# 24 of a decoder layer's 32 gate tiles made in pairs by seven block products, in a stage of their own ahead of the heads

## The chip, the cores and the metric

The kernel runs on one core of a Trainium2 chip. The metric is the device time of one execution in microseconds (us), the median over several runs. The time before is 1961.22 us, the median of 3 runs from 1959.63 to 1961.33. A core has five engines that run side by side, each through its own queue in order: PE (matrix products, with its weight loads as PEld), DVE (VectorE), ACT (ScalarE), POOL (GpSimd) and SP, which here issues most DMAs. Products land in PSUM (8 banks); everything else lives in SBUF, and what does not fit there goes through DRAM.

## The reference

One layer of a decoder: 16 meta tokens and 1024 tokens of width 1024, a token-mixing block of two branches (gated linear attention and mLSTM), merged by two sigmoid gates, then a gated FFN with a short causal convolution. Cut to what matters here:

```python
proj = rms_norm(h) @ w_in + b_in            # 1040 x 1024 by 1024 x 8216
(g_q, g_k, g_v, g_r, g_lr, m_q, m_k, m_v, m_o, m_i, m_f, gate_a, gate_b) = split(proj)
log_a = log_sigmoid(g_lr @ gla_w_gate + gla_b_gate) / 16
o_gla = head_rms(gla_chunked(g_q * s, g_k, g_v, log_a)) * silu(g_r)
o_ml  = head_rms(mlstm_chunked(conv(m_q), conv(m_k), m_v, m_i, log_sigmoid(m_f))) * sigmoid(m_o)
y = sigmoid(gate_a) * (o_gla @ w_branch_gla) + sigmoid(gate_b) * (o_ml @ w_branch_ml)
h = h + y @ w_out
h = h + (silu(gate) * up) @ w_down          # gate, up = conv(rms_norm(h) @ w_up)
```

The gate tiles of the title are the columns of `g_r`, `m_o`, `gate_a` and `gate_b`: 4 x 1024 columns, 32 tiles of 128.

## The kernel before

**Numbers.** Each float32 operand is split into a high part (H) and a low part (L) that PE takes at full rate; a product is three matmuls, H·H, H·L and L·H. The splits cost an ACT copy (H) and a subtraction (L, DVE or POOL).

**Stages.** (1) x is loaded, normalised and transposed into `xH`, `xL` (`norm_x`), while the first projections start. (2) Eight heads, 0 to 3 GLA and 4 to 7 mLSTM. (3) The merge products (`prod3`, L951): `bg` with the GLA outputs `og`, then `bm`. (4) The output projection (`out_product`, L1235). (5) The FFN up-projection (`piece`, `product`, L1149), its convolution and gating (`gate_pair`). (6) The down-projection (`down`, L1365). Stage 5 already makes its tiles in pairs by seven block products: x in 2 x 2 blocks (4 of the 8 k blocks by half of the tokens), the two weight tiles in 2 x 2 blocks, sums of blocks prepared ahead (`combos`, `prep_pair`), then products V, X, Y, Z of 12 matmuls on 258 or 256 columns, some of them added up in one PSUM bank: V, X | Y, Z | X again | Y, Z again, the last two behind the next piece's first four. A pair is two pieces of seven products.

**Main work and side work of a head.** The main work is PE's projections: k and q in three segments each (24 matmuls on about 342 columns, `proj_cm`, L155), v in nine chunks (`proj_v`, L198 and L185, DVE adds the bias), then the gate tiles: two of r (`gate_proj`, L444) and one of gate_a (`merge_gate`, L454), three segments each. ACT evicts k, q and gates from PSUM and adds the bias; r stays in SBUF, gate_a goes to DRAM (`gsc`). After the heads the eight gate_b tiles follow, also to DRAM. The side work is a generator for each head, `gla(s)` or `mlstm(s)`, which works on the k, q and v of the head before: in GLA the decay (`pre`, three products, abs, exp, log and a scan `bc`), seven levels of scores (`level`: DVE differences, ACT exp, POOL products L663, DVE product L664; then the PE product `sc`, L600, and a masked copy by DVE or ACT copies), the chain of states over 8 chunks, and `post` (norm: a power on POOL, L93; scaling, L538; transposes `ot`, L548; the gate r applied, L550; the split of the result and its store to `osc`). `advance()` takes one step of the oldest side generator after each main segment. `small_rows` works out the mLSTM's rows for all heads, once, as a side generator behind GLA head 3.

**Order.** The framework plans the order of each engine's instructions when the kernel is built: by priority, which is the order of the code except where `hp(n)` moves a block ahead by n, and taking what is ready by its own estimate of times. On the chip the order is then fixed, and an engine waits at an instruction whose inputs or buffer are not there.

**Buffers that matter.** Weights: raw tiles in `wr` (2), splits in `wH`, `wL` (3 each). Staging `gst` (1). PSUM in the heads: `pj` 3, `s` 3, `ot` 2 banks. In the heads' pool: `k`, `q`, `v`, `r` 2 each, `w` 5, `of` and `oH` 1 each. When the heads' pool closes, its place is taken by the merge stage's `Y` and `O` tiles (`yg`, `og`).

Of the kernel before, what the change touches and what calls it, by code (L numbers as in the profile page):

```python
# [17 lines left out]
P = 128  # L18
# [27 lines left out]
def hybrid_kernel(ctx, tc, x, meta, norm_mix, w_in, b_in, gla_w_gate, gla_b_gate, gla_norm,  # L46
# [24 lines left out]
    hd = heads_ctx.enter_context(tc.tile_pool(name="hd", bufs=1, side="right"))  # L71
    ps_ctx = heads_ctx.enter_context(ExitStack())
    ps = ps_ctx.enter_context(tc.tile_pool(name="ps", bufs=1, space=PSUM))
# [33 lines left out]
    lrHL = [wp.tile([P, NK, P], F32R, name=f"w{p}_lr", tag="w" + p) for p in "HL"]  # L107
    for t in lrHL:
        nc.vector.memset(t.bitcast(F32), 0.0)
    SMALL = ((0, O_LR, 16), (32, O_MI, 4), (64, O_MF, 4))  # L110

    def prep_small():

        raw = wp.tile([P, T], F32, name="wr_lr", tag="gst", bufs=1)[:, :NK * 24].rearrange("p (k n) -> p k n", k=NK)
        wH, wL = lrHL
# [12 lines left out]
    class Units:  # L128
        def __init__(self):
            self.specs, self.got, self.done = [], {}, 0  # L130
# [5 lines left out]
        def get(self, u, ahead=2):  # L136
            while self.done <= min(u + ahead, len(self.specs) - 1):
# [7 lines left out]
    U = Units()  # L145

# [68 lines left out]
    GATE_LATER = [s < 5 for s in range(8)]  # L215

    def kq_units(s):
        if s in uk:
            return
# [6 lines left out]
    def head_units(s):  # L226
        h = s % 4
        kq_units(s)
        if s == 0:
            uk["lr"] = U.add()  # L230
        uv[s] = u_v((O_GV if s < 4 else O_MV) + DV * h, f"{'gm'[s // 4]}v{h}_")

    def gate_units(s):
        h = s % 4
        o = (O_GR if s < 4 else O_MO) + DV * h
        ur[s] = [u_cm(w_in, o + P * j, f"r{s}_{j}") for j in range(2)]

    head_units(0)
    for s in range(8):
        if GATE_LATER[s]:  # L240
            kq_units(s + 1)
        gate_units(s)
        if s < 7:
            head_units(s + 1)
        uga[s] = u_cm(w_in, O_GA + P * s, f"ga{s}")
    for j in range(NK):
# [5 lines left out]
    xM = hd.tile([P, NK * 48 + 80], F32R, name="xM")  # L252
    nc.gpsimd.memset(xM.bitcast(F32), 0.0)
    gmix = hd.tile([P, D], F32, name="gmix", tag="bc")

    rmask = hd.tile([P, T], F32, name="rmask")
    nc.vector.memset(rmask, 1.0)
    nc.vector.memset(rmask[:, 0:1], 0.0)
    nc.vector.memset(rmask[:, NM:].rearrange("p (n w) -> p n w", w=P)[:, :, 0:1], 0.0)
    A = hd.tile([P, NC, P], F32, name="A", tag="A", bufs=1)  # L260
    nc.vector.memset(A, 0.0)

# [5 lines left out]
    va = hd.tile([P, T], F32, name="va", tag="oH", bufs=1)[:, :P]  # L268
# [15 lines left out]
    wg = hd.tile([NM + 1, 512], F32, name="wg")  # L284
    small.append((wg[0:16, :], gla_w_gate[0]))
    small.append((wg[16:17, :], gla_b_gate))
    vf = hd.tile([P, T], F32, name="vf", tag="r", bufs=2)[:88, :2 * P].rearrange("p (a b) -> p a b", b=P)
    rows(vf[:, 0, :], ffn_conv_w, 0, 88)
    rows(vf[0:44, 1, :], ffn_conv_w, 88 * P, 44)
    rows(vf[44:88, 1, :], ffn_conv_b, 0, 44)  # L290

# [10 lines left out]
    def load_x(*tiles):  # L302
        for i in tiles:
            n = NM if i == 0 else P
            tag, bufs = [("w", 5), ("q", 2), ("k", 2)][(i >= 5) + (i >= 7)]
            xt = hd.tile([P, T], F32, name=f"xt{i}", tag=tag, bufs=bufs)
# [3 lines left out]
    def norm_x(i):  # L310
# [3 lines left out]
        ss = hd.tile([P, 1], F32, name=f"xss{i}", tag="ss1", bufs=3)  # L314
        junk = hd.tile([P, T], F32, name=f"xj{i}", tag="of", bufs=1)
        nc.scalar.activation(junk[:n, :D], xt[:n, :D], AF.Square, accum_out=ss[:n])
        with hp(40):
            v = hd.tile([P, 1], F32, name=f"xv{i}", tag="xv", bufs=3)
            nc.vector.tensor_scalar(v[:n], ss[:n], 1.0 / D, EPS, OP.mult, OP.add)
            rs = hd.tile([P, 1], F32, name=f"xr{i}", tag="xr", bufs=3)  # L320
# [28 lines left out]
    for i in range(4, NC + 1):  # L349
        if i == NC:  # L350
            columns()
        last = norm_x(i)
# [5 lines left out]
    fc = const.tile([P, 4, 44], F32, name="fc")  # L358

    def conv_columns():  # L360
        for i in range(2):
# [1116 lines left out]
```

## Time and profile before

| what | value |
|---|---|
| median of 3 runs | 1961.22 us (1959.63 to 1961.33) |
| the profiled execution's span | 1960.6 us |
| mean granted PE clock | 0.997 of full |
| start of the heads' main work without x tiles to wait for | about 36 us |
| first merge product | 963.65 us |
| HBM read, written | 166.07 MB, 56.71 MB |

How to read the rows that follow. In a row of stretches: from and to (us), length, then busy time and number of instructions of PE, PEld, DVE, ACT and POOL, the granted PE clock, the DMA engines' share and GB/s; with a line or tile chosen, only the engines that ran it. In a group of instructions: line, engine, operation, output<-inputs, shapes, count | busy us, mean ns | idle time before them, and what ended it. In the view of one line: count, ns min/median/max, first and last start. In a timeline: start, length, engine, line, what; in brackets the idle time before it and its releaser. In the waits: who waited for whom, us in all, times, longest. Matmuls overlap in the records (a matmul of 342 columns shows some 320 ns but the next starts 157 ns later), so stretches are used for PE.

### The profile page before, as it was taken

The numbers are of one execution on the slowest core, as the hardware profiler recorded it, in microseconds if no ns is written. First come the engines' busy times: TensorE is split into PE (matmuls) and PEld (weight loads), VectorE is DVE, ScalarE is ACT, GpSimd is POOL, SyncE is SP. The second block draws the span as 40 slices with busy tenths as digits, with TensorE's granted clock in tenths as the row PEclk, the third lists the DMA queues.
The fourth block names the chain that finished last, engine by engine and source line by source line (L and its number), as shares of the span: only waits on it lengthen the run. The fifth ranks groups of instructions, "written<-read, shape, count | busy, mean of one in ns | idle before, by whom it ended". The sixth has DMA issues, their size and how long they took to land. (4 is left out here: it accounts for less than half of the span.)

```text
span 1960.6 us, 31110 instructions
## 1 busy us (share of the span) xinstructions
PE 1925.3 (98%) x13181; PEld 1840.3 (94%) x13181; DVE 965.9 (49%) x1444; ACT 753.4 (38%) x1183; POOL 308.1 (16%) x229
## 2 busy tenths in 40 slices
PE   7999999999999999999999999999999999999998
PEld 6999999999999999999999998999999999978886
DVE  6263636264644434332112447688888888710202
ACT  5243535344634424233311235544445454431211
POOL 3030202020000000000000002012222222364220
PEclk9999999999999999999999999999999999999999
DMA  4211202131323231319952433333333333587721
GB/s 152 57 35 56 76 24 91 29 100 33 104 72 87 67 97 44 98 43 179 327 215 65 136 112 109 119 108 120 113 130 113 122 121 119 172 301 258 244 94 43
DMA packets 191270, 224.79 MB, mean 115 GB/s; under 512 B 11102, under 2 KB 150640, under 8 KB 191131
## 3 DMA queue, kind: packets, MB, share of 16 engines
q1 hardware_dynamic: 190843, 221.76, 36.1%
q8 instruction: 103, 1.69, 0.4%
q10 hardware_dynamic: 288, 1.05, 0.1%
q14 instruction: 36, 0.29, 0.0%
HBM read 166.07 MB, written 56.71 MB: 114 GB/s over the span
## 5 line engine op out<-in xcount | busy, mean ns | idle before, releaser
L1365 PE MATMUL pd<-ringH,a 128*128 128x512 f32 x416 | 131.6, 393 | 2.0 <-DMA a<-adrL 2.0
L155 PE MATMUL pj<-xH,wH_r 128*128 128x342 f32 x384 | 126.1, 328 | 0.0
L155 PE MATMUL pj<-xH,wL_r 128*128 128x342 f32 x384 | 122.9, 320 | 0.0
L155 PE MATMUL pj<-xL,wH_r 128*128 128x342 f32 x384 | 122.6, 319 | 0.0
L1399 DVE TENSOR_TENSOR acc<-pd,acc 128x512 f32<-128x512 f32 x16 | 11.1, 691 | 196.9 <-PE pd L1365 196.9
L1365 PEld LDWEIGHTS pd<-ringH,a 128*128 128x128 f32 x416 | 78.0, 188 | 20.1 <-DMA a<-adrL 2.4
L663 POOL TENSOR_TENSOR pk<-pk,kT 128x256 f32<-128x256 f32 (+1 forms) x40 | 58.8, 1501 | 163.0 <-ACT pk L661 90.5
L1365 PE MATMUL pd<-ringL,a 128*128 128x512 f32 x208 | 82.5, 397 | 1.5 <-POOL ringL L1344 1.5
L198 PE MATMUL pv<-wH_gv,xH 128*128 128x256 f32 x256 | 74.8, 292 | 0.0
L198 PE MATMUL pv<-wH_mv,xH 128*128 128x256 f32 x256 | 74.6, 291 | 0.0
L1235 PE MATMUL po<-wL_wo,yH 128*128 128x256 f32 x256 | 72.0, 282 | 2.0 <-DVE wL_wo L104 2.0
L1235 PE MATMUL po<-wH_wo,yH 128*128 128x256 f32 x256 | 72.8, 284 | 0.9 <-DVE h L1242 0.9
L155 PEld LDWEIGHTS pj<-xH,wH_r 128*128 128x128 f32 x384 | 72.3, 188 | 1.0 <-issue 1.0
L155 PEld LDWEIGHTS pj<-xL,wH_r 128*128 128x128 f32 x384 | 72.3, 188 | 1.0 <-issue 1.0
L155 PEld LDWEIGHTS pj<-xH,wL_r 128*128 128x128 f32 x384 | 72.2, 188 | 0.0
L198 PE MATMUL pv<-wL_gv,xH 128*128 128x256 f32 x256 | 72.0, 281 | 0.0
L198 PE MATMUL pv<-wL_mv,xH 128*128 128x256 f32 x256 | 71.9, 281 | 0.0
L198 PE MATMUL pv<-wH_gv,xL 128*128 128x256 f32 x256 | 71.9, 281 | 0.0
L198 PE MATMUL pv<-wH_mv,xL 128*128 128x256 f32 x256 | 71.9, 281 | 0.0
L1235 PE MATMUL po<-wH_wo,yL 128*128 128x256 f32 x256 | 71.8, 281 | 0.0
L202 DVE TENSOR_TENSOR v<-pv,bB 128x256 f32<-128x256 f32 x64 | 26.8, 420 | 87.3 <-PE pv L198 87.3
L1196 DVE SCALAR_TENSOR_TENSOR cv<-u,fc,cv 128x1024 f32<-128x1024 f32 x44 | 69.4, 1578 | 0.4
(625 smaller groups left out, 6704.3 us busy)
## 6 DMA issues: line engine op xcount, KB each, us to landing
rd<-in_ffn_w_down_dram SPq DMA_DIRECT2D x36, 512.0 KB
rg<-in_ffn_w_up_dram SPq DMA_DIRECT2D x22, 512.0 KB
ru<-in_ffn_w_up_dram SPq DMA_DIRECT2D x22, 512.0 KB
a<-adrH SPq DMA_DIRECT2D x44, 256.0 KB
a<-adrL SPq DMA_DIRECT2D x44, 256.0 KB
adrH<-aH SPq DMA_DIRECT2D x21, 512.0 KB
adrL<-aL SPq DMA_DIRECT2D x21, 512.0 KB
wr_r<-in_w_in_dram SPq DMA_DIRECT2D x16, 512.0 KB
```

The source lines that it names most:

```text
L155: nc.tensor.matmul(pt[:, :n], a[:, k, :], b[:, k, base + t0:base + t0 + n], start=(i == 0), stop=(i == 3 * NK - 1))
L198: nc.tensor.matmul(pt[:, :DV], a[:, k, t0:t0 + P], b[:, k % 4, :], start=(i == 0), stop=(i == 3 * NK - 1))
L202: nc.vector.tensor_tensor(vt[:n, c, :DV], pt[:n, :DV], bB[:n, :], OP.add)
L663: nc.gpsimd.tensor_tensor(e, e, k, OP.mult)
L1196: nc.vector.scalar_tensor_tensor(y, u[:, j:SEQ + j], fc[:, j, jj:jj + 1], y, OP.mult, OP.add)
L1235: nc.tensor.matmul(pt[:, :DV], a, b[:, k % 4, :], start=(k == 0 and i == 0), stop=(k == NK - 1 and i == len(terms) - 1))
L1365: nc.tensor.matmul(pts[t][n], a[:, c], b[:, 512 * n:512 * n + 512], start=start and i == 0, stop=stop and i == 2)
L1399: nc.vector.tensor_tensor(acc[:, h], pts[t][n], acc[:, h], OP.add)
```

## The change

The order of the kernel becomes: x; k and q of head 0; two gate_b tiles (`EARLY`); a gate stage of 12 pairs; the small projection (`lr`, for the decays and the mLSTM's gates) and v of head 0; the heads; six gate_b tiles (`LATE`) as the main work of the last head.

- **The gate stage** makes r of all eight heads (16 tiles) and gate_a (8 tiles) in 12 pairs by seven products, as the FFN does. The sums of blocks of x (`TB`) are made once ahead of it; for the rest it reads `xH`, `xL` in place. Weights are split with the three slots of `wH`, `wL` alone. The results, without bias, are stored to DRAM: r to `rdr`, gate_a to `gsc`.
- **Heads**: main work is k and q and v alone. `load_r(s)` fetches r from DRAM within the side work, and the bias is added in the sigmoid or silu (in the merge stage too). `main(gen, rate)` takes `rate` side steps a segment.
- The decay of a GLA head becomes a function of its own, `decay(s)`, called before `post` of the head before it (for head 0 ahead of its v). Scores of small levels come two levels behind their products instead of one. `post` has one more empty step, `small_rows` two more; `small_rows` runs ahead of GLA head 0.
- **Pools**: tiles that hold x live in a pool `xs` that closes after k and q of head 0; the gate stage's pool `gp` and PSUM pool `psG` follow in its place, then the heads' pool `hd`. k and q of even heads and the masks stay in `keep`. The masks are built in the gate stage, wholly on POOL.

```diff
-    GATE_LATER = [s < 5 for s in range(8)]
+    EARLY, LATE = (0, 1), (2, 3, 4, 5, 6, 7)
...
     def merge_gate(which, j):
-        u = (uga if which == "a" else ugb)[j]
-        c = (C_GA if which == "a" else C_GB) + j
-        if which == "b" and j in (1, 3):
-            st = hd.tile([P, T + 3], F32, name=f"g{which}{j}", tag="k", bufs=2)
+        if j in (3, 5):
+            st = kq_tile(8, "k")
...
-        yield from proj_cm(u, TH_POST, T0, lambda p, t0, n: nc.scalar.activation(
-            st[:, t0:t0 + n], p, AF.Identity, bias=cc(c)))
+        yield from proj_cm(ugb[j], TH_POST, T0, lambda p, t0, n: nc.scalar.activation(st[:, t0:t0 + n], p, AF.Copy))
...
+    def load_r(s):
+        heads[s]["r"] = []
+        for j in range(2):
+            r = hd.tile([P, NP], F32, name=f"r{s}_{j}", tag="r", bufs=2)
+            nc.sync.dma_start(r, rdr[2 * s + j])
+            heads[s]["r"].append(r)
...
-        pk = level(1)
-        yield
-        yield
-        for b in (2, 4, 8, 16, 32, 64):
-            nk = level(b)
...
+        pks = []
+        for b in (1, 2, 4, 8, 16, 32, 64):
+            pks.append(level(b))
+            if b > 2:
+                scores_small(pks.pop(0), b // 4)
             yield
...
+        if s < 3:
+            decay(s + 1)
+            yield
         sc = rstd_of(ss, DV, NC + 1, hd, f"rs{s}")
...
+    for _ in kq_proj(0):
+        pass
+    xs_ctx.close()
...
+    for p in range(2):
+        n = (W0, W1)[p]
+        for kk in range(2):
...
+            for dst, c0, eng in ((ra, T0 + W0 * p, nc.gpsimd), (rc, T0 + 512 + W0 * p, nc.vector)):
+                h, l = (rows(t)[:, :, :, c0:c0 + n].bitcast(F32) for t in (xH, xL))
+                eng.tensor_tensor(dst, h, l, OP.add)
+            nc.vector.tensor_tensor(t12[:, 0], rc[:, 0], ra[:, 0], OP.subtract)
+            nc.vector.tensor_tensor(t34[:, 0], rc[:, 1], rc[:, 0], OP.subtract)
+            nc.vector.tensor_tensor(t12[:, 1], rc[:, 1], t12[:, 0], OP.subtract)
+            nc.vector.tensor_tensor(t34[:, 1], ra[:, 1], t12[:, 1], OP.subtract)
+            for r0, t, eng in ((0, t12, nc.vector), (8, t34, nc.gpsimd)):
+                h, l = (rows(TB[x, p][:, r0:r0 + 8, :]) for x in "HL")
+                nc.scalar.activation(h, t, AF.Copy)
+                last = eng.tensor_tensor(l, t, h.bitcast(F32), OP.subtract)
+
+    for j in EARLY:
+        for _ in merge_gate("b", j):
+            pass
...
+    def block_weights(q):
...
+        a["A11"], a["A12"] = two(rg, "A1")
+        yield
...
+        a["S1"], a["S3"] = two(sa, "SA")
+        yield
...
+        a["S2"], a["S4"] = two(sb, "SB")
+        yield
...
+        nc.sync.dma_start(g_raw, wsrc(w_in, 4, 4, off + P, P))
+        nc.scalar.activation(t[:, 0:4], g_raw, AF.Copy)
+        nc.gpsimd.tensor_tensor(t[:, 4:8], g_raw, t[:, 0:4].bitcast(F32), OP.subtract)
+        yield
...
+    def gate_piece(q, p):
...
+            gout[q] = (gp.tile([P, 2, NA], F32, name=f"goA{q}", tag="oA", bufs=2),
+                       gp.tile([P, 2, 512], F32, name=f"goB{q}", tag="oB"))
...
+        gate_product(V, q, p, "A12", "B21", True, True)
+        gate_product(X, q, p, "A11", "B11", True, True)
+        with hp(PRI_E):
+            nc.scalar.activation(g1, V[:, :n], AF.Copy)
+            nc.vector.tensor_tensor(g1, X[:, :n], g1, OP.add)
+        yield
+        gate_product(Y, q, p, "S1", "T1", True, True)
+        gate_product(Z, q, p, "S3", "T3", True, True)
+        yield
+        gate_product(X, q, p, "S2", "T2", False, True)
+        with hp(PRI_E):
+            nc.scalar.activation(u2, X[:, :n], AF.Copy)
+            nc.vector.tensor_tensor(e2, Y[:, h2], u2[:, h2], OP.add)
+            nc.vector.tensor_tensor(e2, Z[:, h2], e2, OP.add)
+        yield
+        gate_product(Y, q, p, "S4", "B22", False, True)
+        gate_product(Z, q, p, "A22", "T4", False, True)
+        with hp(PRI_E):
+            nc.vector.tensor_tensor(e1, Y[:, h2], u2[:, h2], OP.add)
+            nc.vector.tensor_tensor(g2, Z[:, :n], u2, OP.add)
+        yield
+
+    def gate_store(q):
+        _, dst, i = GP[q]
+        oA, oB = gout.pop(q)
+        nc.sync.dma_start(dst[i:i + 2, :, 0:NA].rearrange("j p t -> p j t"), oA)
+        nc.sync.dma_start(dst[i:i + 2, :, NA:NP].rearrange("j p t -> p j t"), oB)
...
+    for q in range(len(GP)):
+        for p in range(2):
+            g = gate_piece(q, p)
+            next(g)
+            if p == 1:
+                weights_step(q + 1)
+            next(g)
+            if p == 1:
+                weights_step(q + 1)
+            if behind:
+                next(behind)
+            if p == 0 and q:
+                gate_store(q - 1)
+                weights_step(q)
+                weights_step(q)
...
+            next(g)
+            behind = g
...
-    main(head_proj(0))
-    conv_columns()
+    main(lr_proj(), 0)
     for s in range(8):
+        if s == 0:
+            decay(0)
+            side.append(small_rows())
         side.append((gla if s < 4 else mlstm)(s))
-        if s == 3:
-            side.append(small_rows())
-        nxt = head_proj(s + 1) if s < 7 else iter(())
-        if GATE_LATER[s]:
-            main(islice(nxt, 6))
-        main(gate_proj(s))
-        main(nxt)
-        main(merge_gate("a", s))
-    for j in range(NK):
-        main(merge_gate("b", j))
+        rate = (1.45, 1.7, 1.7, 1.7, 1.2, 1.2, 1.2, 1.8)[s]
+        if s == 0:
+            main(v_proj(0), rate)
+        if s < 7:
+            main(kq_proj(s + 1), rate)
+            main(v_proj(s + 1), rate)
+        else:
+            for j in LATE:
+                main(merge_gate("b", j), rate)
     while side:
         advance()
...
-        nc.scalar.activation(y, y, AF.Sigmoid)
+        nc.scalar.activation(y, y, AF.Sigmoid, bias=cc(C_GA + j))
```

More of the change, by code (lines that the diff above doesn't have):

```diff
@@ L420, in head_proj @@
             if s == 0:
[L421 to L422 removed]
+                yield from together(pk, pq)
             else:
@@ L697, in gla @@
         scores_large(pk, 64)
+        load_r(s)
         yield
@@ L830, in mlstm @@
         qh = WB
+        load_r(s)
         yield
```

312 lines of the change are left out of this document (201 added, 111 removed).

## The prediction

> **What bounds the kernel now.** I read the page's busy shares first, then the slices, then stretches of single stages.
>
> ```profile
> span 1960.6 us, 31110 instructions
> PE 1925.3 (98%) x13181; PEld 1840.3 (94%) x13181; DVE 965.9 (49%) x1444; ACT 753.4 (38%) x1183; POOL 308.1 (16%) x229
> ...
> PE   7999999999999999999999999999999999999998
> ...
> DVE  6263636264644434332112447688888888710202
> ...
> PEclk9999999999999999999999999999999999999999
> ```
>
> PE is busy in every slice at full clock, so time goes only where PE work goes, provided that no other engine takes over. A share of 98% could hide idle time inside pipelined matmuls, so I price matmuls by stretches. The first row below holds the L155 matmuls (plain projections) of the stretch that has nothing but plain gate tiles; the second, from the FFN, holds two pairs made of seven block products (2 x 168 matmuls; 338 start in it).
>
> ```profile
> 899.50:963.65 64.15, 64.15 (x408) 64.03 (x408) 1.00 1.02 261
> ...
> 1401.33:1441.41 40.08, 40.08 (x338) 40.08 (x337) 34.39 (x43) 18.97 (x25) 10.22 (x6) 1.00 0.36 119
> ```
>
> Plain: 64.15 us / 408 = 157.2 ns for 342 columns; two tiles are 144 of them, 22.64 us. By seven products, two tiles take 40.08 / 2 = 20.04 us, and the FFN keeps that pace with DVE busy 34.39 of 40.08 us.
>
> One place does lose time, at the end of head 3:
>
> ```profile
> 504.82 3.79 POOL L93 TENSOR_TENSOR rs3r<-rs3v,mhalf 128x9 f32<-128x9 f32 x1 [7.21 <-DVE rs3v L91]
> ...
> L93 POOL TENSOR_TENSOR rs2r<-rs2v,mhalf x1: 1797/1797/1797, 390.8 to 390.8; 128x9 f32<-128x9 f32 x1
> ...
> 509.05 1.59 PE L548 MATMUL ot<-ident,or 128*128 128x128 f32 x4 [3.15 <-DVE or L538]
> ...
> 505.00:510.00 5.00, 1.85 (x11) 1.23 (x9) 3.38 (x6) 4.95 (x5) 3.60 (x1) 0.82 0.00 0
> 510.00:515.00 5.00, 4.88 (x19) 4.84 (x18) 4.94 (x11) 1.10 (x2) 0.00 (x0) 0.50 0.01 4
> 515.00:520.00 5.00, 5.00 (x33) 4.80 (x33) 4.92 (x7) 1.61 (x2) 0.00 (x0) 1.00 0.75 196
> ```
>
> POOL's power for the head's norm takes 3.79 us there and 1.80 in another head; PE sits idle 3.15 us, and then the granted clock is 0.82 and 0.50 for two windows of 5 us. Lost: 3.15 + 5 x 0.18 + 5 x 0.50 = 6.6 us at most; I take 6, as some of the window at 0.82 is the idle time itself. This is also the price of a stall: beyond some 3 us it costs twice itself. The Trainium skill states the same under TensorE: Matmul & The Clock Gate, section "Part 1: The HAM clock gate": an idle window of about 3.4 us drops the array to half clock until a busy window has passed. By that rule the loss is 3.15 + 1.7 = 4.9 us, and the trace, with its longer low window, says somewhat more.
>
> **The change, part by part.**
>
> *Products.* 24 tiles at 22.64 us a pair become 12 pairs at 20.04: 12 x 2.60 = **31.2 us less** on PE. The eight remaining tiles stay plain.
>
> *Stage set-up.* The combinations of x (TB) are built in four quarters, each on 2 x 2 x 257 columns. POOL adds 1028 elements and subtracts 2056; DVE adds 1028, combines 4 x 514 and subtracts 2056; ACT copies 2 x 2056.
>
> ```profile
> L1344 POOL TENSOR_TENSOR ringL<-rd,ringH 128x1024 fp32r<-128x1024 f32 x21 | 51.4, 2460 | 37.9 <-ACT ringH L1343 37.9
> ...
> L104 DVE TENSOR_TENSOR wL_r<-wr_r,wH_r 128x1024 fp32r<-128x1024 f32 x16 | 19.5, 1218 | 5.9 <-ACT wH_r L103 5.9
> L103 ACT ACTIVATE wH_r<-wr_r 128x1024 fp32r<-128x1024 f32 x16 | 16.9, 1056 | 31.8 <-PE pv L198 18.1 <-PE pj L155 13.6
> ...
> 36.59 0.69 DVE L331 TENSOR_TENSOR xL<-xtp,xH 128x512 fp32r<-128x512 f32 x1
> ...
> 36.00:62.00 26.00, 25.88 (x218) 25.88 (x219) 4.11 (x7) 6.97 (x14) 4.37 (x8) 1.00 0.08 22
> ```
>
> At 2.46, 1.22 and 1.06 us per 1024 a quarter costs POOL 7.4, DVE 6.1 and ACT 4.2 us; all four 29.6, 24.5 and 17. What hides them: the last x tile is done at about 37, and from 36 on PE still has two thirds of the 218 matmuls above (q and k; the small projection leaves), 17 us, then two early gate tiles, 22.6, then V and X of the first piece, 2.9: 42 us until the first T block is needed, against 15 us of POOL for the first half. The second half has 10 us more. Cost 0; without the cover it would be the 30 us of POOL.
>
> *Inside the stage.* DVE has less here than in the FFN (no convolution, no gating), and that stage runs at 20.04. Two waits are new. First, three weight slots hold three splits a pair, so SB of pair q takes the slot that the product Y(S4) of pair q-1 has just left, and only Z(A22), 20.04 / 14 = 1.43 us, lies between it and X(S2), which needs the split:
>
> ```profile
> L1109 DVE TENSOR_TENSOR LSB<-SB,HSB 128x1024 fp32r<-128x1024 f32 x17 | 20.5, 1207 | 0.0
> ...
> L1108 ACT ACTIVATE HSB<-SB 128x1024 fp32r<-128x1024 f32 x17 | 18.0, 1060 | 6.5 <-PE Z L1149 6.5
> ```
>
> 1.06 + 1.21 - 1.43 = 0.84 us late, 11 times, 9 us if PE waits in place; 0 if V and X of the next piece, which are ready, are queued first. Second, oB has one buffer, so the e2 sums of pair q wait until pair q-1 is stored:
>
> ```profile
> 868.05 0.34 SPq L456 DMA_DIRECT2D gsca<-ga  x1
> ...
> 873.28 0.55 ACT L454 ACTIVATE gb<-pj,col 128x342 f32<-128x342 f32 x1 [3.06 <-DMA gsca<-ga]
> ...
> DVE of L550 <- DMA oscmL<-of: 21.8, 4, 8.2
> ```
>
> A store of 513 KB is 5.2 us from issue to release. Counted from the end of Y(S4) of q-1: e1 and g2 done at about 2.1, oA issued 2.2, oB 2.5, released 7.7, e2's first sum done 8.2; Y(S4) of q needs that bank after Z, X, V, X, Y, Z, 6 x 1.43 = 8.6. It just fits; a store as late as the 8.2 us in the last row makes it 2.6 us late. Queued behind e2 on DVE are the splits of the next weights, with 5 products of slack. I take 3 us for both waits together (0 to 10).
>
> *Into the heads.* PSUM and SBUF change hands, and the small projection runs before any decay can. Its 72 matmuls (11.4 us) hide the hand-over; the decay of head 0 (next rows: first product 90.4, scan from 98.0, 2.3 long: 10 us) hides under head 0's v, 24 us. I take 2 us (0 to 6).
>
> ```profile
> L623 PE MATMUL pre<-raw_s,wg x24: 447/450/555, 90.4 to 416.3; 17*128 17x346 f32 x16, 17*128 17x348 f32 x8
> ...
> L632 DVE TENSOR_TENSOR_SCAN bc<-rmask,la x4: 2324/2324/2325, 98.0 to 423.6; 128x1040 f32<-128x1040 f32 x4
> ```
>
> *Heads.* They keep all side work and lose nine of their 24 main segments. Both halves of GLA head 1, all engines and then L155 alone, and an mLSTM head:
>
> ```profile
> 198.90:252.00 53.10, 53.07 (x347) 51.38 (x347) 34.08 (x44) 27.66 (x39) 14.50 (x10) 1.00 0.22 60
> 252.00:306.90 54.90, 54.90 (x385) 51.76 (x383) 19.97 (x42) 20.48 (x43) 2.63 (x3) 1.00 0.20 61
> ...
> 198.90:252.00 53.10, 44.02 (x265) 41.61 (x264) 1.00 0.22 60
> 252.00:306.90 54.90, 16.11 (x96) 15.10 (x96) 1.00 0.20 61
> ...
> 525.50:623.00 97.50, 97.50 (x661) 94.39 (x661) 44.81 (x99) 41.98 (x69) 2.21 (x5) 1.00 0.34 94
> ...
> L1123 DVE TENSOR_TENSOR SA<-ru x22: 669/674/692, 1247.8 to 1664.2; 128x512 f32<-128x512 f32 x22
> ...
> L1124 DVE TENSOR_TENSOR SA<-rg,ru x22: 683/1710/1720, 1248.4 to 1665.1; 128x512 f32<-128x512 f32 x22
> ...
> PEld sc L600: 1.6, 4
> ```
>
> A GLA head keeps 108.0 - 3 x 11.32 = 74 us of PE against DVE 54.05 - 3 x 1.22 = 50.4; an mLSTM head 97.5 - 34 = 63.5 against 41. Averages still favour PE. The first half does not: its levels now lie under six segments of k and q, 6 x 44.02 / 11 = 24.0, plus 53.07 - 44.02 = 9 of side matmuls: 33 us, and DVE needs 34.08 less two gate splits, 31.6. That is 96%. The new order (scores two levels behind instead of one) gives it slack, and the second half has 39 us of PE for 19 of DVE to catch up in. I take 5 us over all heads (0 to 8 stalls like the one above, less its clock share: 0 to 25). The stall at 505 itself should go: the small rows, whose scans ran beside that power, move to head 0: **6 us less**. r comes by DMA instead of from PSUM: two loads of 513 KB, asked for steps ahead of `post`, at 60 GB/s of traffic in the rows above: 0.
>
> *End of the heads.*
>
> ```profile
> L456 SPq DMA_DIRECT2D gscb<-gb x8: 319/320/339, 883.7 to 965.2; - x8
> ...
> L935 SPq DMA_DIRECT2D ogL<-oscgL x8: 320/446/713, 924.9 to 956.4; - x8
> ...
> 963.65 0.32 PE L951 MATMUL bg<-ogH,wH_bg 128*128 128x342 f32 x1
> ```
>
> The loads of o took 32 us and were issued 39 us before the first merge product. Now the last head has 6 x 11.32 = 68 us of gates plus 14 of side matmuls, and 17 side steps at 1.8 a segment end about half-way: some 39 us remain, and the first products take k blocks as they land. 0 (0 to 12).
>
> **Sum** against the profiled span: 1960.6 - 31.2 - 6 + 3 + 2 + 5 = 1933.4; the median of the runs stands 0.6 above that span: **1934 us**.
>
> **Rivals.**
>
> *The stage's waits are real* (the oB store or the SB slot). For: one buffer, and the 8.2 us store. Against: PE's queue can take other products first, as FFN pieces already interleave. SB's 9 us and a store half as late as that row, 11 x 1.3 = 14, are 23 in place of 3: 1954 (1945 to 1957). Chance 0.18. With the store 2.6 us late each time and no SB wait, 11 x 2.6 = 29 in place of 3, it is 1960, no change (within 0.2%, 3.9 us, which is what this kernel's runs can tell): 0.06.
>
> *VectorE paces the GLA heads* (slower than before). For: L1124 takes 1.71 us with POOL running and 0.68 without, beside L1123's 0.67. If DVE and POOL kept each other out throughout, the first half would need 31.6 + 14.5 = 46 us against 33 of PE: 13 us late in each of four heads, 52, and four clock drops of 3: 1934 - 5 + 64 = 1993. It decides from 27 / 4, about 7 us a head, on. Against: in the heads of before PE waited for scores 1.6 us in all, and whole segments of the next k, q and v are ready to fill. Chance 0.14.
> The Trainium skill supports this rival: SBUF — State Buffer, "Who interferes with whom", says that a DVE instruction with two SBUF inputs and a GpSimd one that reads SBUF exclude each other for the whole instruction. The rows of L1124 agree; no run so far shows how much of the levels it catches.
>
> *It gains, but the 505 stall or one like it stays*: 1940. That lies in the forecast's own band, 1922 to 1945, chance 0.62 in all.
>
> **How the numbers follow.** Faster 0.62 + 0.18 = 0.80, same 0.06, slower 0.14. Low end: all new costs 0 gives 1924, and a little for the bounds of the pair price, 1923. High end: the waits rival and no change, 1960; that leaves the slower 0.14 and some 0.04 below outside.
>
> **What would show it.** Right: 168 matmuls per gate pair in about 20.0 us with no PE gap at X(S2) or Y(S4); no PE idle time of 2 us or more between 37 us and the first head; GLA head pitch 72 to 77 us, mLSTM 62 to 66; clock 1.00 through the heads; the first merge product about 28 us earlier. Wrong: PE released by DMA rdr or gsca stores or by DVE LSB in the stage, PE idle before `sc` released by DVE or POOL, clock rows of 0.5 in the heads, or merge products that wait for og.

## The result, and the profile after

The changed kernel takes 1980.75 us (median of 4 runs, 1978.71 to 1982.95) against 1960.43 for the kernel before beside it: a ratio of 1.0101, 95% interval 1.0087 to 1.0116. It is slower by 20 us where the forecast had 26 less. First the page of the changed kernel:

```profile
span 1981.2 us, 32109 instructions
PE 1911.6 (96%) x13445; PEld 1819.4 (92%) x13445; DVE 1088.0 (55%) x1638; ACT 756.8 (38%) x1186; POOL 342.5 (17%) x264
...
PE   6899999899998999999999999999999999999998
```

PE has eights where it had only nines: small gaps, spread over the first half. To see where, both kernels in the same stretches, the last one ending at the first merge product (columns as in the forecast: length, busy PE, PEld, DVE, ACT, POOL, granted clock, DMA share, GB/s). Before:

```profile
0.00:60.00 60.00, 47.40 (x347) 44.81 (x348) 31.91 (x71) 29.54 (x58) 20.04 (x43) 1.00 0.41 126
60.00:100.00 40.00, 40.00 (x304) 38.88 (x303) 12.41 (x19) 12.28 (x17) 0.00 (x0) 1.00 0.25 68
100.00:330.00 230.00, 229.46 (x1549) 219.54 (x1548) 119.91 (x190) 102.59 (x171) 43.23 (x32) 1.00 0.20 59
330.00:380.00 50.00, 50.00 (x345) 47.50 (x344) 23.85 (x34) 18.25 (x38) 6.47 (x7) 1.00 0.13 33
380.00:963.65 583.65, 580.03 (x3837) 560.99 (x3836) 238.99 (x444) 233.39 (x390) 30.54 (x31) 0.99 0.36 95
...
508.20:515.00 6.80, 5.83 (x21) 5.38 (x21) 6.30 (x15) 2.87 (x3) 0.40 (x1) 0.50 0.01 3
```

After, and below the dots its stretches at half clock:

```profile
0.00:60.00 60.00, 44.77 (x303) 42.40 (x304) 45.78 (x63) 33.13 (x57) 28.24 (x22) 0.97 0.41 127
60.00:100.00 40.00, 34.08 (x244) 33.10 (x243) 26.77 (x30) 11.68 (x18) 21.38 (x41) 1.00 0.35 103
100.00:330.00 230.00, 227.99 (x1889) 225.55 (x1888) 118.70 (x190) 59.94 (x92) 17.50 (x15) 1.00 0.44 113
330.00:380.00 50.00, 44.92 (x315) 42.61 (x314) 32.29 (x57) 21.60 (x26) 6.63 (x10) 0.93 0.23 66
380.00:976.00 596.00, 576.87 (x3886) 543.42 (x3886) 326.84 (x614) 271.35 (x478) 60.21 (x61) 0.99 0.31 88
976.00:980.66 4.66, 1.47 (x11) 1.19 (x9) 0.37 (x1) 2.09 (x4) 0.00 (x0) 0.89 0.89 261
...
37.60:41.00 3.40, 3.37 (x16) 3.37 (x17) 3.03 (x7) 2.42 (x5) 0.00 (x0) 0.50 0.00 0
368.70:375.50 6.80, 5.83 (x28) 5.67 (x29) 5.29 (x14) 3.24 (x4) 3.78 (x4) 0.50 0.01 1
474.50:477.90 3.40, 2.88 (x12) 2.89 (x13) 3.40 (x4) 1.26 (x2) 2.14 (x2) 0.50 0.02 5
624.70:631.50 6.80, 5.87 (x25) 5.90 (x26) 5.92 (x8) 1.06 (x1) 1.04 (x2) 0.50 0.54 190
904.60:908.00 3.40, 3.40 (x16) 3.40 (x15) 2.54 (x4) 0.00 (x0) 0.00 (x0) 0.50 0.38 95
979.70:986.50 6.80, 5.84 (x20) 5.84 (x21) 1.23 (x1) 0.91 (x2) 0.00 (x0) 0.50 1.03 391
```

This gives the account. In the rows PE's idle time is length less busy: up to the first merge product 50.6 us after, 16.8 before. Half of the busy time at half clock is lost: 10.7 us in the first five windows after, 2.9 in the one of before. What remains of the busy time is work: 919.4 us after, 944.0 before. So by that product 33.8 us of idle time and 7.8 of low clock stand against 24.6 of saved work: 17.0 us later (980.66 against 963.65). Behind it another 3.6 us are lost, 2.9 of them in the last window above. The table lays this beside the forecast's terms:

| place | forecast, us | measured, us (idle + lost at low clock, less before's) |
|---|---|---|
| work of the products | -31.2 | -24.6 |
| up to 60 us (set-up) | 0 | 2.6 + 1.7 = 4.3 |
| 60 to 330 (gate stage) | 3 | 7.4 |
| 330 to 380 (into the heads) | 2 | 5.1 + 2.9 = 8.0 |
| heads, with the stall at 505 | 5 - 6 | 15.5 + 3.2 = 18.7 |
| last gates to first merge product | 0 | 3.2 |
| behind it | 0 | 3.6 |
| sum | -27.2 | 20.6 |

What PE waited for, in the view of waits (total, times, longest):

```profile
PE xtp L320 <- DVE xt L315: 10.8, 2, 10.1
PE sct L608 <- DVE A L632: 6.2, 4, 1.8
PE rtp L512 <- ACT srst L497: 4.5, 1, 4.5
PE msc L827 <- DVE KT L820: 3.9, 2, 2.4
PE bg L1153 <- ACT gb L449: 3.2, 1, 3.2
PE sc L615 <- DVE of L546: 3.0, 1, 3.0
PE ftp L283 <- DVE xL L324: 3.0, 2, 2.7
PE sc L615 <- POOL pk L664: 2.6, 1, 2.6
PE gX L984 <- DVE goA L1005: 2.3, 1, 2.3
...
PE gZ L984 <- ACT gb L449: 1.8, 1, 1.8
...
PE sc L615 <- DVE A L632: 1.3, 1, 1.3
```

Only the first of them, the wait for the first x tile, was there before at such a length. The score products `sc` and the turn `sct` of the four GLA heads wait 13.1 us in all. Each of the others is one late operation, most of them at a place where one stage hands over to the next. The timeline shows four of them:

```profile
29.85 5.45 POOL L916 TENSOR_TENSOR ra<-xH,xL 128x1032 f32<-128x1032 f32 x2
...
33.27 3.11 DVE L315 SCALAR_TENSOR_TENSOR xt<-xt,xr,gmix 128x1024 f32<-128x1024 f32 x1
...
84.80 0.80 ACT L449 ACTIVATE gb<-pj 128x342 f32<-128x342 f32 x2 [9.30 <-DMA gscb<-gb]
...
369.67 1.97 PE L512 MATMUL rtp<-ident,srst 128*128 128x128 f32 x8 [4.50 <-ACT srst L497]
...
472.58 4.05 POOL L664 TENSOR_TENSOR pk<-pk,kT 128x256 f32<-128x256 f32 x3 [3.46 <-ACT pk L662]
475.02 1.22 PE L615 MATMUL sc<-pk 128*128 128x128 f32 x4 [2.60 <-POOL pk L664]
```

The sums of x (`ra`, part of the TB set-up) run on POOL while DVE still scales the last x tile (3.11 us there). The second early gate's eviction waits 9.3 us for the store of the first: both use the one `gst` buffer. The rows' transposes stand in PE's queue before their input is ready. And with 2.6 us of waiting at a score product come 3.4 us at half clock, from 474.5.

### The profile page after: what moved, and what is told of

It is laid out like the page before. It is cut to its first block, busy times and chain, and to the rows that moved or that the text cites. A ratio compares the mean times of both kernels' runs of the same rounds, so it can differ in the third digit from the quotient of the medians.

```text
span 1981.2 us, 32109 instructions
## 1 busy us (share of the span) xinstructions
PE 1911.6 (96%) x13445; PEld 1819.4 (92%) x13445; DVE 1088.0 (55%) x1638; ACT 756.8 (38%) x1186; POOL 342.5 (17%) x264
## 5 line engine op out<-in xcount | busy, mean ns | idle before, releaser
L1437 PE MATMUL po<-wH_wo,yH 128*128 128x256 f32 x256 | 72.8, 284 | 0.9 <-DVE h L1444 0.9
L664 POOL TENSOR_TENSOR pk<-pk,kT 128x256 f32<-128x256 f32 (+1 forms) x40 | 47.2, 1202 | 148.3 <-ACT pk L662 114.5
L200 PE MATMUL pv<-wL_gv,xH 128*128 128x256 f32 x256 | 72.8, 284 | 0.0
L1153 PE MATMUL bg<-ogH,wH_bg 128*128 128x342 f32 x192 | 62.6, 328 | 4.3 <-ACT gb L449 3.2
L1329 POOL TENSOR_TENSOR SB<-SA,rg 128x512 f32<-128x512 f32 x20 | 26.5, 1325 | 232.5 <-ACT u L1372 96.7
L157 PE MATMUL pj<-xH,wH_gb 128*128 128x342 f32 x192 | 62.8, 327 | 1.9 <-ACT gb L449 1.9
L1153 PE MATMUL bg<-ogL,wH_bg 128*128 128x342 f32 x192 | 62.4, 326 | 0.0
L1153 PE MATMUL bg<-ogH,wL_bg 128*128 128x342 f32 x192 | 62.2, 325 | 0.0
L157 PE MATMUL pj<-xH,wL_gb 128*128 128x342 f32 x192 | 61.7, 322 | 0.0
L157 PE MATMUL pj<-xL,wH_gb 128*128 128x342 f32 x192 | 61.6, 321 | 0.0
```

The source lines that it names most:

```text
L157: nc.tensor.matmul(pt[:, :n], a[:, k, :], b[:, k, base + t0:base + t0 + n], start=(i == 0), stop=(i == 3 * NK - 1))
L200: nc.tensor.matmul(pt[:, :DV], a[:, k, t0:t0 + P], b[:, k % 4, :], start=(i == 0), stop=(i == 3 * NK - 1))
L664: nc.gpsimd.tensor_tensor(e, e, k, OP.mult)
L1153: nc.tensor.matmul(pt[:, i, :n], a[:, k, :], b[k][:, t0:t0 + n], start=(k == 0 and j == 0), stop=(k == NK - 1 and j == 2))
L1329: late.tensor_tensor(sb[:, 0:4], sa[:, 0:4], rg[:, 0:4], OP.subtract)
L1437: nc.tensor.matmul(pt[:, :DV], a, b[:, k % 4, :], start=(k == 0 and i == 0), stop=(k == NK - 1 and i == len(terms) - 1))
```

## The experiments

Three theories: C, the levels of a GLA head have more VectorE work than six segments of k and q cover; L, VectorE and GpSimd keep each other out; B, single late operations at the hand-overs. Each edit is against the changed kernel. The runs of one kernel spread by some us (the changed kernel's four by 4.2), and e2, e3, e4 and e9 have two runs each, with intervals that overlap the changed kernel's 1.0087 to 1.0116: the sizes of their gains or losses are rough, and what they show rests on their traces.

**e1: cover.** Two pairs fewer; their four gate_a tiles are plain ones in the GLA heads (side rates lowered to match).

```diff
-    GP += [(O_GA + 2 * P * j, gsc["a"], 2 * j) for j in range(4)]
+    GP += [(O_GA + 2 * P * j, gsc["a"], 2 * j) for j in range(2)]
...
             main(kq_proj(s + 1), rate)
+            if s < 4:
+                main(merge_gate("a", 4 + s), rate)
```

> Ten pairs in the gate stage instead of twelve; gate_a tiles 4 to 7 are plain again, one as main work between k, q and v of each GLA head, with fewer side steps a segment (1.42 instead of 1.7, 1.29 in head 0). PE gets 2 x 2.6 = 5 us more. Theory C (the score levels of a GLA head have more DVE work than six segments of k and q cover, so PE comes to the products sc and sct too early): PE's waits at sc and sct fall from 13.1 us in all to under 4, and the clock stays at 1.00 from 380 to 700 us (some 5 us): about 1981 + 5 - 14 = 1972. Theory L (DVE and POOL keep each other out, and the stretched instructions are late whatever the cover): waits about halved, 1980. Theory B (the loss is in single buffers and one late chain elsewhere, each with a clock drop): nothing won, 1986.

1970.78 us, ratio 1.0049 (1.0034 to 1.0065): 10 us gained with 5.2 us more of products. No wait at `sc` is left, 5.5 us at `sct`; both windows of low clock in the levels are gone. For C. But the waits at the hand-overs stay. The profile is of a run of 1967.44 us, and the eight runs go from 1963.79 to 1974.09: five of them have a mean granted clock of 0.990 or 0.991, against 0.994 in this one, so that no low clock is left in the levels is shown for this run alone.

**e2: the levels' products on VectorE.**

```diff
-                    nc.gpsimd.tensor_tensor(e, e, k, OP.mult)
+                    nc.vector.tensor_tensor(e, e, k, OP.mult)
```

> The products of the levels that POOL makes (L664, b over 1) go to DVE; nothing else changes. Theory L: without POOL beside it no DVE instruction of the levels is stretched, the waits at sc and sct fall from 13.1 us to 3 or less, about 1967. Theory C: DVE has some 4.5 us more in each GLA head's first half, the waits grow to 20 us or more with more clock drops, about 1990. Theory B: 1981, waits as before.

1975.35 us, ratio 1.0078 (1.0049 to 1.0107): 5 us gained, neither C's loss nor all of L's gain. One line of the levels, the product with q (count, shortest/median/longest ns), first in the changed kernel, then here:

```profile
L665 DVE TENSOR_TENSOR pk<-pk,qT x28: 668/700/1774, 360.7 to 641.5; 128x512 f32<-128x512 f32 x28
```

```profile
L665 DVE TENSOR_TENSOR pk<-pk,qT x28: 664/685/699, 362.1 to 640.4; 128x512 f32<-128x512 f32 x28
```

Without GpSimd beside it none takes over 0.70 us, where some took 1.77. VectorE's busy time stayed the same (1088.0 and 1087.6 us) with 40 more operations: the stretching had cost it as much as the products themselves. So the stretching that L speaks of is real. But the waits at `sc` and `sct` fall only from 13.1 to 10.1 us where L had 3 or less, so it is a small part of them; the gain of 5 us is rough, with two runs.

**e3: slower side steps in k and q** (1.2 a segment, 2.05 in v).

```diff
-            main(kq_proj(s + 1), rate)
-            main(v_proj(s + 1), rate)
+            main(kq_proj(s + 1), 1.2 if s < 4 else rate)
+            main(v_proj(s + 1), 2.05 if 0 < s < 4 else rate)
```

> The same side steps, spread in another way: 1.2 a segment during k and q of heads 1 to 4 instead of 1.45 or 1.7, 2.05 a chunk during v of heads 2 to 4 instead of 1.7. No PE or DVE work is added. Theory C: the waits at sc and sct fall from 13.1 us to 5 or less and the clock drops at 474 and 625 us go: about 1968 to 1972; new waits in the chain of states could take some of it back. Theory L: half of that, 1976. Theory B: 1981.

1985.87 us, ratio 1.0131 (1.0102 to 1.0161): no gain. Waits of 6.9 us at the turn and 4.8 at `sc` remain, 11.7 in place of 13.1, and those at `msc` grew from 3.9 to 6.3. All three theories missed. Why the slower steps didn't help wasn't traced.

**e4: four single waits.** A staging buffer of its own for the second early gate, the first early gate's weight load behind x, four more steps ahead of the rows' transposes (and a higher rate in head 0 for them), KT in the `w` pool.

```diff
-        if j in (3, 5):
+        if j == 1:
+            st = gp.tile([P, 2, NA], F32, name="gb1", tag="oA", bufs=2).rearrange("p a b -> p (a b)")
+        elif j in (3, 5):
...
+        yield
+        yield
+        yield
+        yield
...
-        KT = hd.tile([P, T], F32, name=f"KT{s}", tag="of", bufs=1)
+        KT = wtile(f"KT{s}")
```

> Four single waits are taken away and the rest is left: the second early gate tile is staged in an oA tile instead of the one gst buffer; the weights of the first early gate tile are asked for behind the last x tiles; the transposes of the small rows come four side steps later (1.62 a segment in head 0 for it); KT of the mLSTM heads has a w tile instead of the one of tile that waits for a store. Theory B: gone are the waits at gb, gZ and gX (6 us), rtp (4.5), msc (3.9) and ftp (3), and the clock drops at 37, 368 and 904 us (7 us): about 1959. Theories C and L: the waits at sc and sct stay at 13 us, and no more than half of this comes back: 1970.

1975.23 us, ratio 1.0077 (1.0048 to 1.0106). The waits at `gZ`, `ftp`, `rtp` and `msc` nearly go (0.7 us left at `rtp`, 0.3 and 0.4 at `gZ` and `ftp`), but one of 4.7 us comes up at `sc`, for the copies of the same rows out of the same PSUM banks, and one of 2.1 us at the last x tile's transposes, with the window of low clock at 37 still there. Six us gained in place of 22.

**e5: less for VectorE.** One product of each level left out.

```diff
-            nc.vector.tensor_tensor(pl, pl, lv(qv, b)[:, :, 1, :], OP.mult)
             return pk
```

> The changed kernel without the product of q in a level of scores (the last VectorE operation of each level): the GLA scores lack the factor q, everything else is kept. VectorE has 26.9 us less in the four GLA heads (28 operations of 960 ns), nearly 7 us less in each half that holds the levels; TensorE's work is unchanged. Theory C (in the levels VectorE has more to do than six segments of k and q cover): its 95% in those halves falls to about 75%, the 13.1 us of waits ahead of the score products and of the turn fall below 3, the low clock at 475 and 625 goes: 1981 - 10 - 5 = 1966 us. Theory B (the loss sits at the hand-overs between stages): the waits in the levels are a small part, the time stays at 1976 to 1981. Theory L (exclusion by GpSimd): the stretching goes on with the operations that are left, 1974.

1973.65 us, ratio 1.0057 (1.0035 to 1.008): 7 us, half of C's 15. The waits at `sc` and `sct` fall from 13.1 to 6.2, but two windows of low clock remain in the levels, 6.8 us from 478 and 3.4 from 621, where C had none.

**e6: cover moved.** Late gate tiles 2, 4 and 6 go into GLA heads 1 to 3 (side rates lowered there, as in e1).

```diff
-    EARLY, LATE = (0, 1), (2, 3, 4, 5, 6, 7)
+    EARLY, LATE, MOVED = (0, 1), (3, 5, 7), {2: 2, 3: 4, 4: 6}
...
             main(kq_proj(s + 1), rate)
+            if s + 1 in MOVED:
+                main(merge_gate("b", MOVED[s + 1]), rate)
```

> The changed kernel with the same work, but three of the six late gate tiles moved from the last head into GLA heads 1, 2 and 3, between k,q and v of the next head; the last head keeps three. No product is added (ten pairs with four plain tiles in their place cost 5.2 us more in the first experiment). Theory C: the score waits of three heads go as in the first experiment, 8 us and two low-clock windows of 5 us together: 1981 - 13 = 1968, less up to 10 if the last head's own work is then not covered (its loads of o end about 5 us ahead of the first merge product): 1968 to 1978. Theory B: 1976 to 1981, with the waits at the hand-overs as they are.

2010.62 us, ratio 1.0249 (1.022 to 1.0279), worse than either theory had it. Its waits:

```profile
PE bg L1157 <- DMA ogH<-oscgH: 29.8, 1, 29.8
PE sct L610 <- DVE A L634: 14.0, 4, 6.4
```

Three tiles are too little cover for the last head: the merge stands 29.8 us for the loads of o. The forecast's statement that this end costs nothing rested on all six. In the heads the wait only moved to the turn.

**e7: hand-overs.** The rows behind GLA head 0, the columns behind k and q of head 0 (its side rates adjusted), `gst` as in e4.

```diff
-            columns()
-            conv_columns()
+            columns()
...
+    conv_columns()
     xs_ctx.close()
...
-            side.append(small_rows())
         side.append((gla if s < 4 else mlstm)(s))
+        if s == 0:
+            side.append(small_rows())
```

> The changed kernel with three places outside the levels mended: the rows for the mLSTM heads behind GLA head 0 instead of ahead of it, the transposes of the convolution's columns behind k and q of head 0 instead of among the last x tiles, and a staging buffer of its own for the second early gate tile. Theory B: the waits of 4.5 us (transposes of the rows) and 3.0 us (columns), 4.5 us in the first pair, and the low clock at 37 and at 369 (5 us of work) go: 1981 - 17 = 1964 us. Theory C: these waits go too, but the levels' 13 us and their two windows of low clock stay, and head 0 has more side work later: 1968 to 1974.

1998.13 us, ratio 1.0186 (1.0156 to 1.0215). A mending that did harm: VectorE's first sum of the TB set-up starts at 54.8 us in place of 38.2, right behind the columns' copy, and in the first pair PE waits 11.7 us at `gX`. The sum takes a place in the x pool, which the columns' input holds open, and it also stands behind that copy in VectorE's queue; which of the two held it wasn't separated. The rows' transposes, 96 us later, wait 4.6 us again.

**e8: e2, e4's KT, e6 and e7 together.**

> All that helped together: three late gate tiles moved to GLA heads 1 to 3, the products of the levels on VectorE, a buffer of its own for the second early gate tile, the mLSTM's KT in a buffer of the work pool, the small rows behind GLA head 0, the columns behind k and q of head 0. If the losses are what the theories C and B say together, they add: 1981 - 13 - 17 - 5 = 1946 us, below the kernel before (1960). If waits only move on to the next late thing, 1965 to 1972.

2007.90 us, ratio 1.0236 (1.0206 to 1.0265): the faults of e6 and e7 are both there (30.4 us at `bg`, 11.7 at `gX`). It says nothing of whether the gains add.

**e9: x's sums on VectorE.**

```diff
-            for dst, c0, eng in ((ra, T0 + W0 * p, nc.gpsimd), (rc, T0 + 512 + W0 * p, nc.vector)):
+            for dst, c0, eng in ((ra, T0 + W0 * p, nc.vector), (rc, T0 + 512 + W0 * p, nc.vector)):
```

> The changed kernel with one engine exchanged in the set-up of the stage: the sums of x's H and L for the blocks' first operand (two additions of 2.7 to 3.3 us on GpSimd) are made by VectorE. In the profile of the changed kernel the scaling of the last x tile on VectorE takes 3.11 us beside such a GpSimd addition of 2.72 us, 1.24 us elsewhere, and TensorE then waits 3.0 us at the columns' transposes and has a window of low clock at 37. Theory S (the set-up, costed at nothing, is in the way of the last x tiles): the scaling takes 1.24 again, the 3.0 us and the 3.4 us window go, k and q of head 0 end 3 to 4 us earlier: 1977 us. If the wait has another cause (x tiles loaded later than before), nothing moves: 1981.

1976.35 us, ratio 1.0087 (1.0066 to 1.0107), as theory S said. The scaling of x, and the first product of the stage (count, ns, first and last start), with that of the changed kernel below:

```profile
L315 DVE SCALAR_TENSOR_TENSOR xt<-xt,xr,gmix x9: 1273/1278/1286, 8.4 to 32.4; 128x1024 f32<-128x1024 f32 x8, 16x1024 f32<-16x1024 f32 x1
...
L984 PE MATMUL gV<-xH,HgA x96: 277/281/415, 72.8 to 310.8; 128*128 128x258 f32 x48, 128*128 128x256 f32 x48
```

```profile
L984 PE MATMUL gV<-xH,HgA x96: 278/282/288, 79.4 to 316.3; 128*128 128x258 f32 x48, 128*128 128x256 f32 x48
```

No scaling takes 3.11 us any more, and the gate stage begins at 72.8, 6.6 us earlier. 4.4 of them reach the end; the wait at `gX` in the first pair grows from 2.3 to 4.3 us.

**e10 and e11: six mendings, with and without e1's cover.** e2, e9, `gst` and KT of e4, two late gates staged in q's tile, and the rows' transposes three steps later in the `ot` PSUM banks instead of the `s` banks of the scores. The side rates are adjusted here and in e12 to e14 as well.

```diff
+        elif j in (4, 6) and which == "b":
+            st = kq_tile(8, "q")
...
-            tp = ps.tile([P, 4, P], F32, name=f"rtp{g}", tag="s", bufs=3)
+            tp = ps.tile([P, 4, P], F32, name=f"rtp{g}", tag="ot", bufs=2)
```

> The first experiment's kernel (ten pairs, four plain gate_a tiles between k,q and v of the GLA heads) with six mendings: the products of the levels on VectorE, a buffer of its own for the second early gate tile, two of the late ones staged in q's tile, the mLSTM's KT in the work pool, x's sums on VectorE, and the rows' transposes three side steps later with PSUM banks of their own. Of the first experiment's 1971: the transposes' wait 4.5 and its window 3.4, the columns' 2.9 and 3.4 at the start, the first pair's 3 and 3.4, the last eviction's 3 to 5, KT's 1, the levels' 5: 22 to 26 us less, 1945 to 1950, faster than the kernel before (1960), if the waits don't come back at the next late operation as they did in the fourth and eighth experiments; then 1960 to 1970.

> The changed kernel (twelve pairs, no plain tile in the GLA heads) with the same six mendings as its neighbour. Theory C (the levels need cover): it stays behind its neighbour by what the first experiment gained, some 10 us, though it has 5 us less of products, with 5 to 10 us of waits at the score products and the turn left: 1957 to 1962. Theory B (single late operations alone): it is ahead of its neighbour by the 5 us of products: 1940 to 1945.

1965.37 us, ratio 1.0033 (1.002 to 1.0046), with the cover, and 1965.13, ratio 1.0028 (1.0017 to 1.0039), without. Fifteen us better than the changed kernel, not yet as fast as before. e10 lies in the worse of its two ranges; e11 missed both theories, as the two kernels are level: here the cover is worth just the 5.2 us of products that it costs. In both a wait of 4 us stands in the first pair, with 6.8 us at half clock behind it; e11's timeline names it:

```profile
79.84 0.69 DVE L961 TENSOR_TENSOR gSA<-gu 128x512 f32<-128x512 f32 x1 [3.89 <-DMA gu<-in_w_in_dram]
...
84.25 0.58 PE L991 MATMUL gX<-TBH,HgSB 128*128 128x258 f32 x1 [4.12 <-DVE goA L1012]
```

VectorE stands 3.89 us at a sum for the second pair, whose weights have not landed; the sums that the first pair needs are queued behind it.

**e12, e13, e14: three more mendings**, to both, and to e13 with e5's product left out. The second pair's sums come behind the first piece's; the turn comes one step, the rows' transposes two steps later.

```diff
+        with tc.issue_after(GA["first"].ins) if q == 1 else ExitStack():
+            nc.vector.tensor_tensor(sa[:, 0:4], ru[:, 0:4], ru[:, 4:8], OP.add)
+            nc.vector.tensor_tensor(sa[:, 4:8], rg[:, 0:4], ru[:, 0:4], OP.subtract)
...
+        yield
         turn()
```

> The kernel of e10 (ten pairs, four plain tiles in the GLA heads, six mendings) with three more: the first sums of the second pair's weights on VectorE come behind the first piece's sum (in e11 VectorE sat 3.9 us before them for a weight load, and TensorE 4.1 us behind it, with 6.8 us of low clock), the turn one side step later, the rows' transposes two more. e10 had 10.5 us of waits at the turn, 4.2 in the first piece and 13.6 us of low clock there and at 441. If each wait is one late operation: 1965 - 4 - 8 - 6 = 1947 us. If the waits only move to the next late operation: 1960 to 1965.

> The kernel of e11 (twelve pairs, no plain tile in the GLA heads) with the same three mendings. Theory B (single late operations): 4.1 us in the first piece with 3.4 of work at low clock, 3.4 at the rows' transposes with 1.7: 1965 - 12 = 1953 us, level with its neighbour or ahead by some us. Theory C (the levels need cover): the waits at the score products (7.6 us in e11) grow as the rest gets earlier, 1957 to 1963, behind its neighbour.

> The kernel of e13 without the product of q in a level (the GLA scores lack the factor q), 27 us of VectorE less in the four GLA heads. Theory C: what is left of the waits at the score products goes (7.6 us in e11) with their low clock: 10 us below e13. Theory B: within 4 us of e13.

e12: 1951.33 us, ratio 0.9953 (0.9938 to 0.9967). e13: 1956.0, ratio 0.9976 (0.9967 to 0.9986). e14: 1952.2, ratio 0.9956 (0.9941 to 0.9971). All are faster than the kernel before, by 0.2 to 0.5%, and e12 is the fastest. It lies between its two forecasts, nearer to 1947. e13 is 3 us above B's 1953, but behind its neighbour, as C said; e14 is 3.8 us below e13, within B's 4. Below, e12's stretch to its first merge product, and its longest waits ahead of it:

```profile
0.00:949.58 949.58, 921.14 (x6590) 881.69 (x6590) 530.91 (x965) 396.97 (x674) 74.51 (x101) 1.00 0.36 98
```

```profile
PE sct L619 <- DVE A L643: 4.8, 3, 1.8
PE sc L626 <- DVE of L557: 3.0, 2, 2.0
```

e13, some of the stretches that were shown of the changed kernel, then its longest waits at the levels:

```profile
60.00:100.00 40.00, 38.64 (x297) 38.43 (x296) 26.69 (x33) 13.11 (x20) 23.26 (x40) 1.00 0.43 105
...
323.00:373.00 50.00, 46.93 (x341) 44.52 (x340) 33.70 (x56) 22.95 (x29) 0.00 (x0) 1.00 0.30 82
373.00:948.00 575.00, 562.54 (x3835) 528.85 (x3834) 322.98 (x641) 270.21 (x477) 19.29 (x27) 1.00 0.32 87
```

```profile
PE sc L624 <- DVE of L555: 5.0, 3, 2.1
PE sc L624 <- DVE pk L674: 3.5, 5, 1.2
```

Neither kernel has a stretch at half clock ahead of the merge, where the changed kernel lost 10.7 us so. In e13 the idle time of the first pair's stretch falls from 5.9 to 1.4 us, of the entry to the heads from 5.1 to 3.1, of the heads from 19.1 to 12.5. The mendings are worth 25 us together (1980.75 less 1956.0), B's and L's shares in one. Cover is still worth something: e12 leads by 4.7 us though it has 5.2 more of products (its idle time to the merge is 28.4 us; e13's is 952.57 less 919.03, 33.5), and the slowest of its four runs, 1951.89, is faster than the fastest of e13's ten, 1954.62. Less work for VectorE is worth 3.8 us (e14). The intervals of e13 and e14 overlap. C is a part, not the whole: the cover's worth, the products that it costs added back, was 15 us in e1, 5 between e10 and e11, and 10 here (4.7 + 5.2).

## Why the prediction was wrong

- **"31.2 us less" for the products**: nearly right. The pitch of the steady pairs is 20.37 us, by nine pairs of the changed kernel:

```profile
121.53:304.83 183.30, 182.42 (x1515) 180.59 (x1513) 97.84 (x153) 48.27 (x72) 11.59 (x9) 1.00 0.46 115
```

  183.30 / 9 against the forecast's 20.04; 12 x (22.64 - 20.37) = 27.2. The 0.33 a pair too much are mostly the first wait of the point after next, which the overlapping records of matmuls count as busy. The account has 24.6; where the last 2.6 lie wasn't traced.
- **"6 us less" at 505**: right. No wait for that power and no window of low clock is left there.
- **The stage's two waits, 3 us**: right for the steady pairs. PE's weight loads wait for the split of SB, as the forecast feared, but 0.30 us a pair and not 0.84:

```profile
PEld gX L984 <- DVE LgSB L948: 3.3, 11, 0.3
```

  For the store of `oB` VectorE waits twice, 2.1 us in all, and PE not at all that shows. The rival that made the two waits 23 us fell. The first pair wasn't costed: 5.9 us of idle time between 60 and 100, from the `gst` store (e4 removes the wait at `gZ`) and from VectorE's queue (e11, e13). That buffer's store wait stood quoted in the forecast, for a place where it cost nothing.
- **"Cost 0" for the set-up**: the step that failed first. POOL's 5.45 us were covered by PE's work, as the forecast counted, but they lay beside VectorE's scaling of the last x tile, which sets PE's next input. e9: the stage begins 6.6 us earlier with the sums elsewhere.
- **"I take 2 us" into the heads**: 8. The forecast moved the stall at 505 away with the small rows, and didn't ask what covers their chain at its new place, 9 v segments: the transposes wait 4.5 us and the clock halves for 6.8.
- **"I take 5 us over all heads"**: the largest miss. The heads lost 18.7 us more than before although the stall at 505 was gone, where 5 - 6 were forecast. The 96% of the level half was in the text; that "the new order gives it slack" did not hold, as `sc` and `sct` wait 13.1 us, with 4.4 lost at half clock, and KT's wait for `of` (3.9) is besides.
- **"0" at the end of the heads**: 3.2 us and the window behind it. The loads were early enough, as said (with three tiles less, in e6, they are not); the last evictions were not, again for `gst`.
- **"Beyond some 3 us it costs twice itself"**: the bound was too high. In the changed kernel the six waits of 2.4 us and more behind the start all have a window of low clock with them: 18.5 us of waits, and another 13.6 lost at half clock.

The slower rival, VectorE pacing the GLA heads, had the sign and one mechanism of three. Its price was too high in place (13 us in each head; 13.1 in all four) and its exclusion was confirmed in kind: the Trainium skill, SBUF — State Buffer, "Who interferes with whom", holds that a VectorE operation with two inputs in SBUF and a GpSimd one that reads SBUF exclude each other, and L665 (1.77 us beside GpSimd, 0.70 without) and L315 (3.11 and 1.28) agree. The other half of the loss is waits of 2 to 5 us, each at another place, none of which the sum priced together with the low clock that follows it.

What stays open: e12 is still 17 us above the forecast, 5.2 of them by its two pairs fewer. 28.4 us of PE's idle time ahead of the merge remain there, against 16.8 before.

## What to carry to other kernels

Ask of every moved step what it lies beside, not only whether its length is covered: work that PE's time covers can still hold up the one engine that makes PE's next input, by stretching its operations, through a single staging buffer or in an in-order queue. Price waits of 2.4 us and more at up to 1.7 times their length (18.5 us became 32.1 here) and then sum them over all hand-overs. When plain products are replaced by cheaper ones, the side work that they covered becomes the bound in that stretch; keeping a few plain ones there can be faster.

## What the runs showed of the hardware

- The length of a wait didn't decide alone whether the clock was halved with it. One wait of the FFN is 2.2 us long in every kernel. In the changed kernel it lies in a window at half clock (first two rows); in e12 it doesn't (last row; the granted clock is 1.00 from 1262 to 1270):

```profile
1294.21 0.58 PE L1351 MATMUL Y<-BH1t,HSA 128*128 128x256 f32 x1 [2.21 <-ACT BH1t L1291]
...
1293.70:1297.10 3.40, 2.89 (x13) 2.89 (x14) 3.40 (x5) 1.52 (x2) 0.00 (x0) 0.50 0.00 0
```

```profile
1263.35 0.39 PE L1367 MATMUL Y<-BH1t,HSA 128*128 128x256 f32 x1 [2.21 <-ACT BH1t L1307]
```

  Likewise the 2.28 us at the first pair's `gX` had no low clock in the changed kernel and 6.8 us of it in e1, whose 3.0 us at the first merge product had none. So e12, whose waits behind the start are 2.2 us at most and whose clock is full ahead of the last matmuls, may owe a part of that to chance. The Trainium skill, TensorE: Matmul & The Clock Gate, "Part 1: The HAM clock gate", puts the idle window at about 3.4 us; here less sufficed.
- The windows of the changed kernel up to the merge start 331.1, 105.8, 150.2, 279.9 and 75.1 us apart, which is 97, 31, 44, 82 and 22 times 3.413 us: they begin on one grid. They are 3.4 or 6.8 us long, in e7 also 10.2, and 34.1 in e6 over the wait of 29.8. That a wait's place on this grid decides between the cases above would fit, but wasn't tested.
- Taking work from GpSimd and giving it to VectorE left VectorE's busy time as it was (e2: 40 operations more, 1087.6 us against 1088.0).
